# Sample keys in runs of 1 KB, scores by 64x32 products, cache loads on GpSimd's queue

## The chip, the cores and the metric

One NeuronCore of a Trainium2 chip runs the whole program as one launch. The metric is the device time of that launch in microseconds (us); lower is better. The kernel before has a median of 2021.78 us over three runs (2021.5 to 2022.62).

## What is computed

One step of a one-layer decoder for two groups of requests that share the weights: a prompt of 256 new tokens, and 8 sample requests of 8 tokens each. A layer is a mixer (retention beside a short gated convolution), cross-attention to 256 memory tokens, and a SwiGLU FFN, all in fp32 with a model width of 2048. The change touches only the cross-attention of the sample requests, whose memory keys and values come from a cache in DRAM:

```python
q = (h @ w_xq).reshape(B, T, XA_HEADS, XA_DIM)          # 4 heads of 512
s = einsum('bthd,bnhd->bhtn', q, mk) * XA_DIM ** -0.5   # mk, mv: (8, 256, 4, 512) from the cache
p = softmax(s)
o = einsum('bhtn,bnhd->bthd', p, mv)
x + o @ w_xo
```

For the prompt, mk and mv are products of the memory tokens with w_mk and w_mv, and are outputs too.

## The kernel before, in words

Every large product is done three times over on parts: a weight tile is loaded raw (SP's queue, 512 KB a load, L109), split into a high part by ACT (L121) and a remainder by DVE (L122), and multiplied as high x high, high x low and low x high (`mm3`, L162 to L165). `Weights` walks one list of all weight tiles, four raw buffers and five pairs of parts deep, with loads and splits three ahead. One call of its `next()` gives one *chunk*: 12 matmuls of 320 columns in most stages, 6 matmuls of 512 columns in the memory key and value products.

The order of all instructions on TensorE, ACT and DVE is written out by hand. Everything that is not a large product is a Python generator in the queue `background`. After each chunk, `tick(rate)` (L207) adds `rate` to a credit of at most two and runs the front generator for one step, that is to its next `yield`, per whole credit. `drain()` (L217) runs the queue to its end at once.

The cross-attention stage starts at L726. First the query product (8 groups of 8 chunks, rate RATE_XQ after the first group, L972 to L987), whose background is the norm table, `memory_tiles` (transposes of the prompt's memory, L779) and, from groups 1 and 3 on, `sample_head(0)` and `sample_head(1)`. Then, for each of four heads, the memory key and value products (16 chunks each, rate 1, L993 to L1008); heads 2 and 3 of the samples are appended at their own head, and the prompt's own attention of each head (`prompt_scores`, `prompt_values`, 8 and 5 steps) is put at the front of the queue. Last, 12 chunks of the output product (L1012), the drain (L1013) and the rest of that product, which needs the result of all heads.

`sample_head(h)` (L845) takes its requests in two halves p, of four requests j each. Per half: four key tiles (512 KB) are transposed in 32x32 blocks by DVE, one a step, each followed by `fetch_keys()`, which asks for the tile three places on; two empty steps; 16 score matmuls (L860), four requests side by side on column tiles of 32. After the second half the first four value tiles are asked for (`load_values`, L809), the exponents and their sums are made, three steps later the weights are transposed (L876), two steps later 16 value matmuls (L887) run; the second value tiles are asked for, and PACE = 5 steps later the second 16. Keys and values share four `kt` buffers, so a value load waits until the matmuls before have read the buffer. All of these loads are issued by SP, in one order with the weight loads. `OUT` is GpSimd (POOL), which issues the stores of results.

The key load puts partition 32i+q on 128 elements of the head dimension (i) and key q of 32: runs of 512 B.

Of the kernel before, what the change touches and what calls it, by code (L numbers as in the profile page):

```python
# [11 lines left out]
F32 = mybir.dt.float32  # L12
# [24 lines left out]
RATE_RET, RATE_XQ, RATE_KV = 0.9, 1.0, 1.0  # L37
PACE = 5
# [97 lines left out]
def step_kernel(ctx, tc, a, o):  # L136
# [15 lines left out]
    def uid(s):  # L152
        count[0] += 1
        return f"{s}_{count[0]}"
# [284 lines left out]
    with tc.tile_pool(name="ret", bufs=2, reuse_waits="tile") as ret:  # L439
# [162 lines left out]
        for pair in range(4):  # L602
# [27 lines left out]
            if pair == 0:  # L630
                loading.close()
                hold_b = ctx.enter_context(tc.tile_pool(name="hold_b", bufs=1, side="right",
                                                        reuse_waits="tile"))
                b_hi = hold_b.tile([P, KT, T], F32R, name="b_hi")
                b_lo = hold_b.tile([P, KT, T], F32R, name="b_lo")
                hold_b.tile([P, 120], F32, name="fill_b")
# [89 lines left out]
    with tc.tile_pool(name="att", bufs=1, reuse_waits="tile") as att:  # L726
        q_p = att.tile([P, KT, TP], F32, name="q_p")
        q_s = att.tile([P, KT, 80], F32, name="q_s")
        G.memset(q_s[:, :, 64:80], 0.0)
# [23 lines left out]
        def fetch_keys():  # L753


            if not key_order:
                return
            h, b = key_order.popleft()
            src = a["cache_mem_k"][0, b, :, h]
            t = att.tile([P, 8, P], F32, tag="keys", name=uid("keys"), bufs=3)  # L760
            for i in range(4):
                DMA.dma_start(out=t[32 * i:32 * i + 32],
                              in_=src[:, P * i:P * i + P].rearrange("(n q) d -> q n d", q=32))
            keys.append(t)
# [3 lines left out]
        def fetch_memory():  # L768


            i = mem_order.popleft()
            t = att.tile([P, 8, P], F32, tag="keys", name=uid("mem"), bufs=3)
            for d in range(4):
                DMA.dma_start(out=t[32 * d:32 * d + 32].rearrange("p (n m) d -> p n (m d)", n=2),
                              in_=a["mem_prompt"][0, 64 * i:64 * i + 64, XD * d:XD * d + XD]
                              .rearrange("(n q) d -> q n d", q=32))
            keys.append(t)

        def memory_tiles():  # L779
            for i in range(4):  # L780
                t = keys.popleft()
                kt = kv_tile().rearrange("p (n k q) -> p n k q", k=KT, q=32)
                V.transpose(out=kt, in_=t.rearrange("p (n m) d -> p n (m d)", n=2)  # L783
                            .rearrange("p n (c k) -> p n k c", k=KT))
                flat = t.rearrange("p (n m) d -> p n (m d)", n=2)
# [58 lines left out]

        def sample_head(h):  # L845
            ss = mix_tile()
            for p in range(2):
                kts = []
                for j in range(4):
                    kt = kv_tile().rearrange("p (n d c) -> p n d c", d=4, c=32)  # L850
                    V.transpose(out=kt, in_=keys.popleft().rearrange("p n (d c) -> p n d c", c=32))  # L851
# [13 lines left out]
            vs = load_values(h, 0)  # L865
            e, rc = exponents(ss, "s")
# [5 lines left out]
            for _ in range(3):  # L872
                yield
# [98 lines left out]
        for g in range(8):  # L972
            for i, ps in enumerate(product(a_hi, a_lo, KT, RATE_XQ if g else 1.0)):
                k = 2 * g + i
                V.tensor_tensor(out=q_p[:, k, :], in0=ps[:, 0:TP], in1=r_tab[:, 0:TP], op=ALU.mult)
                h, i = divmod(k, 4)
                for d in range(4):
# [14 lines left out]
        att.tile([P, 8], F32, name="fill_a")  # L992
        for h in range(XH):  # L993
            if h > 1:
                background.append(sample_head(h))
# [120 lines left out]
```

## Time and profile before

| what | value |
|---|---|
| median of three runs | 2021.78 us (2021.5 to 2022.62) |
| the profiled execution | 2018.07 us, of which the span in the trace is 2016.3 us |
| TensorE busy | 1985.9 us, 98% of the span |
| DVE, ACT, POOL busy | 1076.1 us (53%), 840.9 us (42%), 123.5 us (6%) |
| DMA | 340.94 MB, mean 169 GB/s |

A busy engine is one with an instruction in flight; matmuls are pipelined, so their recorded times overlap and a busy stretch need not run at full rate. Idle time is put down to what ended it. [...]

### The profile page before, as it was taken

To read this page: it belongs to the slowest core of one execution; us is meant where nothing else is said; L and a number is where in the kernel's file an instruction comes from. 1 tells how busy PE (TensorE), PEld (TensorE's weight loads), DVE (VectorE), ACT (ScalarE), POOL (GpSimd) and SP (SyncE) were. 2 spreads that over 40 slices of the span, in tenths; PEclk is the share of its full clock that TensorE was granted. 3 is DMA by queue.
4 is the path that set the end of the run, shared out by engine and by line. 5 is a ranking of instruction groups with operands and counts; after the bars stand their busy time and mean duration, and the time that the engine had idled before them with its cause. 6 is when DMAs were issued, how large, how long until landed. Compare 5 with 4: busy or idle time off the path is not lost.

```text
span 2016.3 us, 34017 instructions
## 1 busy us (share of the span) xinstructions
PE 1985.9 (98%) x13310; PEld 1907.1 (95%) x13310; DVE 1076.1 (53%) x1931; ACT 840.9 (42%) x1648; POOL 123.5 (6%) x230
## 2 busy tenths in 40 slices
PE   9999999999999999999999999999999999999997
PEld 8999999999998878778899999999999999999997
DVE  5556666555566545556454545544454544545433
ACT  6444433334454345444344434333343433334444
POOL 1111111110110000000010000000000000000010
PEclk9999999999999999999999999999999999999999
DMA  6465555445559965878545444444444444444443
GB/s 211 144 194 158 184 172 162 147 152 174 157 157 252 241 237 187 220 249 260 167 138 160 140 154 152 148 152 151 151 146 147 151 153 153 141 156 150 134 146 115
DMA packets 327664, 340.94 MB, mean 169 GB/s; under 512 B 13132, under 2 KB 296640, under 8 KB 327504
## 3 DMA queue, kind: packets, MB, share of 16 engines
q1 hardware_dynamic: 324240, 329.72, 53.1%
q0 software_dynamic: 3264, 9.05, 1.3%
q8 instruction: 104, 1.70, 0.4%
q14 instruction: 56, 0.46, 0.1%
HBM read 327.11 MB, written 11.61 MB: 168 GB/s over the span
## 4 chain that ended last, share of the span: by engine, by line
PE 92%; DMA 4%; DVE 2%; issue 1%; ACT 1%; SPq 0%; POOL 0%; POOLq 0%; DVEq 0%; ACTq 0%
PE acc L163 29%; PE acc L165 29%; PE acc L164 29%; DMA keys<-in_cache_mem_k_dram 2%; DMA kt<-in_cache_mem_v_dram 2%; PE mix L887 1%; PE mix L860 1%; DVE w_lo L122 1%; PE mix L375 0%; PE mix L165 0%; PE mix L163 0%; PE mix L164 0%; DVE kt L783 0%; DVE kt L851 0%; DMA x_tok<-in_x_prompt_dram 0%
## 5 line engine op out<-in xcount | busy, mean ns | idle before, releaser
L122 DVE TENSOR_TENSOR w_lo<-w_raw,w_hi 128x512 fp32r<-128x512 f32 x1072 | 711.6, 693 | 505.6 <-ACT w_hi L121 504.1
L121 ACT CAST w_hi<-w_raw 128x512 fp32r<-128x512 f32 x1072 | 631.2, 619 | 593.9 <-PE acc L164 520.9
L163 PE MATMUL acc<-a_hi,w_hi 128*128 128x320 f32 x2112 | 660.1, 313 | 3.4 <-ACT w_hi L121 3.1
L165 PE MATMUL acc<-a_hi,w_lo 128*128 128x320 f32 x2112 | 653.9, 310 | 0.7 <-DVE w_lo L122 0.7
L164 PE MATMUL acc<-a_lo,w_hi 128*128 128x320 f32 x2112 | 653.3, 309 | 0.0
L163 PE MATMUL acc<-b_hi,w_hi 128*128 128x320 f32 x1664 | 514.5, 309 | 0.0
L165 PE MATMUL acc<-b_hi,w_lo 128*128 128x320 f32 x1664 | 514.3, 309 | 0.0
L164 PE MATMUL acc<-b_lo,w_hi 128*128 128x320 f32 x1664 | 514.3, 309 | 0.0
L163 PEld LDWEIGHTS acc<-a_hi,w_hi 128*128 128x128 f32 x2112 | 397.1, 188 | 11.2 <-issue 5.3
L165 PEld LDWEIGHTS acc<-a_hi,w_lo 128*128 128x128 f32 x2112 | 397.2, 188 | 1.9 <-DVE w_lo L122 1.9
L164 PEld LDWEIGHTS acc<-a_lo,w_hi 128*128 128x128 f32 x2112 | 397.4, 188 | 0.8
L163 PEld LDWEIGHTS acc<-b_hi,w_hi 128*128 128x128 f32 x1664 | 312.4, 188 | 0.1
L164 PEld LDWEIGHTS acc<-b_lo,w_hi 128*128 128x128 f32 x1664 | 312.4, 188 | 0.0
L165 PEld LDWEIGHTS acc<-b_hi,w_lo 128*128 128x128 f32 x1664 | 312.4, 188 | 0.0
L298 POOL TENSOR_TENSOR sq_sum<-sq_sum,sq_t 128x320 f32<-128x320 f32 x43 | 38.3, 891 | 1125.7 <-ACT sq_t L297 1125.7
L164 PE MATMUL acc<-w_lo,b_hi 128*128 128x512 f32 x256 | 100.6, 393 | 3.3 <-DVE w_lo L122 3.3
L163 PE MATMUL acc<-w_hi,b_hi 128*128 128x512 f32 x256 | 102.5, 400 | 0.0
L165 PE MATMUL acc<-w_hi,b_lo 128*128 128x512 f32 x256 | 100.2, 391 | 0.0
L707 DVE TENSOR_TENSOR x_res<-x_res,acc 128x320 f32<-128x320 f32 x80 | 37.7, 486 | 74.9 <-PE acc L165 74.9
L163 PEld LDWEIGHTS acc<-w_hi,b_hi 128*128 128x128 f32 x256 | 48.4, 189 | 14.2 <-issue 5.0
L164 PEld LDWEIGHTS acc<-w_lo,b_hi 128*128 128x128 f32 x256 | 48.4, 189 | 13.4 <-DVE w_lo L122 4.4
L165 PEld LDWEIGHTS acc<-w_hi,b_lo 128*128 128x128 f32 x256 | 48.4, 189 | 10.4
(226 smaller groups left out, 1017.4 us busy)
## 6 DMA issues: line engine op xcount, KB each, us to landing
w_raw<-in_w_in_dram SPq DMA_DIRECT2D x112, 512.0 KB, 4.1
w_raw<-in_w_gate_dram SPq DMA_DIRECT2D x88, 512.0 KB, 4.1
w_raw<-in_w_up_dram SPq DMA_DIRECT2D x88, 512.0 KB, 4.3
w_raw<-in_w_down_dram SPq DMA_DIRECT2D x80, 512.0 KB, 3.3
w_raw<-in_w_mix_out_dram SPq DMA_DIRECT2D x32, 512.0 KB, 4.5
w_raw<-in_w_xq_dram SPq DMA_DIRECT2D x32, 512.0 KB, 5.0
keys<-in_cache_mem_k_dram SPq DMA_DIRECT2D x128, 128.0 KB, 5.2
kt<-in_cache_mem_v_dram SPq DMA_DIRECT2D x32, 512.0 KB, 7.5
```

The source lines that it names most:

```text
L121: self.nc.scalar.copy(out=hi, in_=src)
L122: self.nc.vector.tensor_tensor(out=lo, in0=src, in1=hi.bitcast(F32), op=ALU.subtract)
L163: PE.matmul(out, ah, bh, start=start, stop=False)
L164: PE.matmul(out, ah, bl, start=False, stop=False)
L165: PE.matmul(out, al, bh, start=False, stop=stop)
L298: G.tensor_tensor(out=sq, in0=sq, in1=t, op=ALU.add)
L707: V.tensor_tensor(out=x_res[:, m, :], in0=x_res[:, m, :], in1=ps[:, 0:T], op=ALU.add)
L860: PE.matmul(ss[32 * j:32 * j + 32, NM * p:NM * p + NM] .rearrange("q (n c) -> q n c", c=32), q_s[:, 4 * h + d, 16 * j:16 * j + 32], kts[j] ...
L887: PE.matmul(os[32 * j:32 * j + 32, :], pts[:, n, p, 32 * j:32 * j + 32], vs[j][:, n, :], start=(p == 0 and n == 0), stop=(p == 1 and n == ...
```

## The change

- A key tile is loaded in runs of 256 elements (1 KB): partition 64i+32s+q holds key half i, head-dimension half s, and key q of 32, with four groups m of 32 keys beside each other.
- The score product of a half becomes 64 matmuls, each on 64 rows and 32 columns of the array (8 pieces e of the head dimension, 2 key halves i, 4 requests j) with 128 columns streamed; the two key halves go to two PSUM banks. The queries are kept on 64 partitions per head, scaled by DVE at the start of a sample head and copied to the other 64 by ACT (the scaling by POOL at L982 goes). The softmax works on the two banks.
- Keys and values are asked for on POOL's queue instead of SP's.
- PACE goes; V_TICKS = 10 steps lie between each request for values and its use, and the value matmuls of a half are cut into two steps of eight.
- RATE_XQ is 1.15 instead of 1.0, and sample heads 2 and 3 enter the queue one head earlier.
- Two unused filler tiles go.

The diff, cut to its core:

```diff
-RATE_RET, RATE_XQ, RATE_KV = 0.9, 1.0, 1.0
-PACE = 5
+RATE_RET, RATE_XQ, RATE_KV = 0.9, 1.15, 1.0
+V_TICKS = 10
...
-        q_s = att.tile([P, KT, 80], F32, name="q_s")
-        G.memset(q_s[:, :, 64:80], 0.0)
+        q_s = att.tile([P, 16, 64], F32, name="q_s")
+        q_rep = att.tile([P, 528], F32, name="q_rep")
+        G.memset(q_rep[:, 512:528], 0.0)
...
-            t = att.tile([P, 8, P], F32, tag="keys", name=uid("keys"), bufs=3)
-            for i in range(4):
-                DMA.dma_start(out=t[32 * i:32 * i + 32],
-                              in_=src[:, P * i:P * i + P].rearrange("(n q) d -> q n d", q=32))
+            t = att.tile([P, 1024], F32, tag="keys", name=uid("keys"), bufs=3)
+            for i in range(2):
+                for s in range(2):
+                    at = 64 * i + 32 * s
+                    OUT.dma_start(out=t[at:at + 32].rearrange("q (m d) -> q m d", d=256),
+                                  in_=src[P * i:P * i + P, 256 * s:256 * s + 256]
+                                  .rearrange("(m q) d -> q m d", q=32))
...
-                DMA.dma_start(out=t, in_=a["cache_mem_v"][0, 2 * j + p, :, h]
+                OUT.dma_start(out=t, in_=a["cache_mem_v"][0, 2 * j + p, :, h]
...
+        def sample_exponents(pair):
+            mxs = [att.tile([P, 2], F32, tag=f"mxs{i}", name=uid("mx")) for i in range(2)]
+            sv = [ps[:, 0:256].rearrange("p (t n) -> p t n", n=P) for ps in pair]
+            for mx, v in zip(mxs, sv):
+                V.tensor_reduce(out=mx, in_=v, axis=AX.X, op=ALU.max, negate=True)
+            V.tensor_tensor(out=mxs[0], in0=mxs[0], in1=mxs[1], op=ALU.min)
...
+            for t in range(2):
+                for i, v in enumerate(sv):
+                    S.activation(out=e[:, t, P * i:P * i + P], in_=v[:, t, :], func=AF.Exp,
+                                 bias=mxs[0][:, t:t + 1], scale=1.0, accum_out=sm[:, i, t:t + 1])
...
         def sample_head(h):
-            ss = mix_tile()
+            mine, other = (slice(64 * i, 64 * i + 64) for i in (h // 2, 1 - h // 2))
+            V.tensor_tensor(out=q_rep[mine, 0:512].rearrange("p (e t) -> p e t", t=64),
+                            in0=q_s[mine, 8 * (h % 2):8 * (h % 2) + 8, :],
+                            in1=r_tab[mine, TP:T].unsqueeze(1).to_broadcast([64, 8, 64]),
+                            op=ALU.mult)
+            S.copy(out=q_rep[other, 0:512], in_=q_rep[mine, 0:512])
+            ss = [mix_tile() for _ in range(2)]
...
-                for d in range(4):
-                    for j in range(4):
-                        PE.matmul(ss[32 * j:32 * j + 32, NM * p:NM * p + NM]
-                                  .rearrange("q (n c) -> q n c", c=32),
-                                  q_s[:, 4 * h + d, 16 * j:16 * j + 32], kts[j][:, :, d, :],
-                                  start=(d == 0), stop=(d == 3), tile_position=(0, 32 * j),
-                                  skip_group_check=True)
+                for e in range(8):
+                    for i in range(2):
+                        half = slice(64 * i, 64 * i + 64)
+                        for j in range(4):
+                            PE.matmul(ss[i][32 * j:32 * j + 32, P * p:P * p + P]
+                                      .rearrange("q (m c) -> q m c", c=32),
+                                      q_rep[half, 64 * e + 16 * j:64 * e + 16 * j + 32],
+                                      kts[j][half, :, e, :], start=(e == 0), stop=(e == 7),
+                                      tile_position=(64 * i, 32 * j), skip_group_check=True)
             vs = load_values(h, 0)
-            e, rc = exponents(ss, "s")
+            e, rc = sample_exponents(ss)
...
-            for _ in range(3):
+            for _ in range(4):
                 yield
...
-            for _ in range(2):
+            for _ in range(V_TICKS - 4):
                 yield
             os = mix_tile()
             for p in range(2):
...
+                    yield
                 if p == 0:
                     vs = load_values(h, 1)
-                    for _ in range(PACE):
+                    for _ in range(V_TICKS):
                         yield
...
-                    S.copy(out=q_s[32 * i:32 * i + 32, 4 * h + d, 0:64],
-                           in_=ps[32 * d:32 * d + 32, TP:T])
-                if i == 3:
-                    for d in range(4):
-                        G.tensor_tensor(out=q_s[:, 4 * h + d, 0:64], in0=q_s[:, 4 * h + d, 0:64],
-                                        in1=r_tab[:, TP:T], op=ALU.mult)
+                    S.copy(out=q_s[at:at + 32, place + d, :], in_=ps[32 * d:32 * d + 32, TP:T])
...
-            if h > 1:
-                background.append(sample_head(h))
+            if 0 < h < 3:
+                background.append(sample_head(h + 1))
```

The first `yield` added at the value matmuls stands after the eight matmuls of one n, inside the loop over n.

## Rows read from the trace of the kernel before

**Rows 1.** The page, part 1: busy time, share of the span and instructions by engine.

```profile
PE 1985.9 (98%) x13310; PEld 1907.1 (95%) x13310; DVE 1076.1 (53%) x1931; ACT 840.9 (42%) x1648; POOL 123.5 (6%) x230
```

**Rows 2.** Table by stretches: from:to, length, busy by engine, PEclk, DMA share, GB/s.

```profile
616.00:704.00 88.00, 82.95 (x610) 71.39 (x609) 48.57 (x78) 33.89 (x89) 2.31 (x8) 1.00 0.97 248
...
1090.00:1980.00 890.00, 890.00 (x6078) 889.93 (x6077) 431.44 (x719) 347.21 (x633) 9.70 (x11) 1.00 0.47 149
```

**Rows 3.** Table by stretches, four holes of TensorE in the cross-attention stage.

```profile
602.00:605.00 3.00, 1.49 (x9) 0.96 (x8) 1.06 (x2) 2.87 (x10) 1.15 (x4) 1.00 0.45 128
635.00:638.00 3.00, 1.85 (x11) 1.33 (x10) 1.02 (x2) 2.88 (x9) 1.15 (x4) 1.00 1.19 203
...
694.00:699.00 5.00, 3.66 (x40) 2.09 (x35) 2.91 (x6) 3.29 (x11) 0.00 (x0) 1.00 1.13 219
...
834.00:849.00 15.00, 11.62 (x69) 8.35 (x67) 9.86 (x14) 4.34 (x9) 0.72 (x1) 1.00 1.15 238
```

**Rows 4.** Table by stretches, the five us behind the last of these holes.

```profile
849.00:854.00 5.00, 5.00 (x20) 4.21 (x20) 4.03 (x6) 2.49 (x4) 0.00 (x0) 0.66 1.10 283
```

**Rows 5.** TensorE's timeline around value bursts: start, length, instruction [idle before it].

```profile
649.80 0.31 PE L165 MATMUL acc<-a_hi,w_lo 128*128 128x320 f32 x1
...
...
657.62 0.41 PE L163 MATMUL acc<-a_hi,w_hi 128*128 128x320 f32 x1
...
666.37 0.31 PE L165 MATMUL acc<-a_hi,w_lo 128*128 128x320 f32 x1
...
668.53 0.41 PE L163 MATMUL acc<-a_hi,w_hi 128*128 128x320 f32 x1
...
706.81 0.31 PE L165 MATMUL acc<-a_hi,w_lo 128*128 128x320 f32 x1
...
713.39 0.50 PE L163 MATMUL acc<-w_hi,b_hi 128*128 128x512 f32 x1
...
873.68 0.39 PE L164 MATMUL acc<-w_lo,b_hi 128*128 128x512 f32 x1
873.90 0.39 PE L165 MATMUL acc<-w_hi,b_lo 128*128 128x512 f32 x1
...
879.94 0.50 PE L163 MATMUL acc<-w_hi,b_hi 128*128 128x512 f32 x1
...
966.85 0.31 PE L165 MATMUL acc<-a_hi,w_lo 128*128 128x320 f32 x1
...
970.25 1.90 PE L887 MATMUL mix<-kt,pts 128*32 128x512 f32 x10 [0.43 <-DMA kt<-in_cache_mem_v_dram]
972.83 0.66 PE L908 MATMUL mix<-ident,misc 128*128 128x128 f32 x4 [0.68 <-ACT misc L896]
```

**Rows 6.** SP's timeline: start, length, the issues of the last values.

```profile
959.93 1.99 SPq L813 DMA_DIRECT2D kt<-in_cache_mem_v_dram  x4
```

**Rows 7.** Groups of instructions on POOL: its DMA issues, busy us and mean ns.

```profile
L549 POOL DMA_DIRECT2D out_ret_s_dram<-sn x8 | 7.4, 924 | 73.4 <-DVE sn L545 73.4
L523 POOL DMA_DIRECT2D out_ret_p_dram<-sp x8 | 5.0, 622 | 19.0 <-ACT sp L522 19.0
...
L1007 POOL DMA_DIRECT2D out_mk_dram<-kv x4 | 3.0, 750 | 108.7 <-ACT kv L1006 108.7
```

**Rows 8.** DMA issues: queue, count, KB each, median us from issue to landing.

```profile
keys<-in_cache_mem_k_dram SPq DMA_DIRECT2D x128, 128.0 KB, 5.2
...
out_mk_dram<-kv POOLq DMA_DIRECT2D x4, 512.0 KB, 5.7
```

**Rows 9.** Table by stretches, while key loads land.

```profile
641.00:645.00 4.00, 4.00 (x28) 4.00 (x28) 2.81 (x7) 2.57 (x7) 0.00 (x0) 1.00 1.20 200
```

**Rows 10.** TensorE's timeline and one line's instructions: matmuls on column tiles of 32.

```profile
624.53 1.94 PE L860 MATMUL mix<-kt,q_s 128*32 128x256 f32 x32
...
88.58 0.65 PE L500 MATMUL mix<-s,qm 128*32 128x128 f32 x16
...
L802 PE MATMUL mix<-ssq_mem,own x8: 171/182/193, 611.6 to 611.7; 128*32 128x2 f32 x8
```

More of the change, by code (lines that the diff above doesn't have):

```diff
@@ L635, in step_kernel @@
                 b_lo = hold_b.tile([P, KT, T], F32R, name="b_lo")
-                hold_b.tile([P, 120], F32, name="fill_b")
             background.append(iter((None,)))
@@ L771, in fetch_memory @@
             i = mem_order.popleft()
-            t = att.tile([P, 8, P], F32, tag="keys", name=uid("mem"), bufs=3)
+            t = att.tile([P, 1024], F32, tag="keys", name=uid("mem"), bufs=3)
             for d in range(4):
-                DMA.dma_start(out=t[32 * d:32 * d + 32].rearrange("p (n m) d -> p n (m d)", n=2),
+                DMA.dma_start(out=t[32 * d:32 * d + 32].rearrange("p (n d) -> p n d", n=2),
                               in_=a["mem_prompt"][0, 64 * i:64 * i + 64, XD * d:XD * d + XD]
@@ L782, in memory_tiles @@
                 kt = kv_tile().rearrange("p (n k q) -> p n k q", k=KT, q=32)
-                V.transpose(out=kt, in_=t.rearrange("p (n m) d -> p n (m d)", n=2)
-                            .rearrange("p n (c k) -> p n k c", k=KT))
-                flat = t.rearrange("p (n m) d -> p n (m d)", n=2)
+                flat = t.rearrange("p (n d) -> p n d", n=2)
+                V.transpose(out=kt, in_=flat.rearrange("p n (c k) -> p n k c", k=KT))
                 for n in range(2):
@@ L843, in part @@
             return ap.rearrange("p (j r) -> p j r", r=r)[:, :, 8 * p:8 * p + 8]
-        def sample_head(h):
-            ss = mix_tile()
+        def sample_exponents(pair):
[4 more added lines that the diff above has]
+            V.tensor_tensor(out=mxs[0], in0=mxs[0], in1=mxs[1], op=ALU.min)
+            e = misc_tile().rearrange("p (t n) -> p t n", n=NM)
+            sm = att.tile([P, 2, 2], F32, tag="sms", name=uid("sm"))
+            for t in range(2):
+                for i, v in enumerate(sv):
+                    S.activation(out=e[:, t, P * i:P * i + P], in_=v[:, t, :], func=AF.Exp,
+                                 bias=mxs[0][:, t:t + 1], scale=1.0, accum_out=sm[:, i, t:t + 1])
+            rc = att.tile([P, 2], F32, tag="rcs", name=uid("rc"))
+            V.tensor_tensor(out=rc, in0=sm[:, 0, :], in1=sm[:, 1, :], op=ALU.add)
+            V.reciprocal(out=rc, in_=rc)
+            return e, rc
+        def sample_head(h):
+            mine, other = (slice(64 * i, 64 * i + 64) for i in (h // 2, 1 - h // 2))
[5 more added lines that the diff above has]
+            ss = [mix_tile() for _ in range(2)]
             for p in range(2):
@@ L849, in sample_head @@
                 for j in range(4):
-                    kt = kv_tile().rearrange("p (n d c) -> p n d c", d=4, c=32)
-                    V.transpose(out=kt, in_=keys.popleft().rearrange("p n (d c) -> p n d c", c=32))
+                    kt = kv_tile().rearrange("p (m e c) -> p m e c", e=8, c=32)
+                    V.transpose(out=kt, in_=keys.popleft().rearrange("p (m e c) -> p m e c", e=8, c=32))
                     fetch_keys()
@@ L976, in step_kernel @@
                 h, i = divmod(k, 4)
+                at, place = 64 * (h // 2) + 32 * (i // 2), 8 * (h % 2) + 4 * (i % 2)
                 for d in range(4):
-                    S.copy(out=q_s[32 * i:32 * i + 32, 4 * h + d, 0:64],
-                           in_=ps[32 * d:32 * d + 32, TP:T])
-                if i == 3:
-                    for d in range(4):
-                        G.tensor_tensor(out=q_s[:, 4 * h + d, 0:64], in0=q_s[:, 4 * h + d, 0:64],
-                                        in1=r_tab[:, TP:T], op=ALU.mult)
+                    S.copy(out=q_s[at:at + 32, place + d, :], in_=ps[32 * d:32 * d + 32, TP:T])
             if g == 1:
@@ L990, in step_kernel @@
             background.appendleft(sample_outputs(h, osb))
-        att.tile([P, 8], F32, name="fill_a")
         for h in range(XH):
-            if h > 1:
-                background.append(sample_head(h))
+            if 0 < h < 3:
+                background.append(sample_head(h + 1))
             for dst, prompt_part in ((o["mk"], prompt_scores), (o["mv"], prompt_values)):
```

## The prediction

> **What bounds the kernel now.** I read the page first: TensorE is busy for 98% of the span [rows 1], so only two things can move the time: what TensorE has to do, and the holes and stretched bursts in it. Next the table by stretches: the FFN stretch has no hole (890.00 of 890.00 us, 6078 matmuls, so 0.146 us each), while 616 to 704 us loses 5.05 of 88 us with the DMA engines at 0.97 [rows 2]. The change only touches the stage from 572 to 977 us (query product, memory keys and values, start of the output product), so I read that stage's holes one by one. Four of them are a split (ACT and DVE, L121 and L122) that came late because a key load, or a weight load behind it on SP's queue, came late: 1.51, 1.15, 1.34 and 3.38 us, together 7.38 [rows 3]. [...]
>
> The value bursts are the largest item, and busy time hides most of it. A clean burst of 16 recorded matmuls lets the main product go on 2.16 us after the last main matmul (666.37 to 668.53). Where the values are late, it dribbles: a few matmuls per landed tile, with ten left when the last one lands at 970.25, and each stretch counts as busy. From the last main matmul to the next it takes 649.80 to 657.62 = 7.82 us in head 0, 706.81 to 713.39 = 6.58 in head 1, 873.90 to 879.94 = 6.04 in head 2 [rows 5]. Less 2.16 each, that is 5.66 + 4.42 + 3.88 = 13.96 us. Head 3 pays at its second burst: 966.85 to 972.83 is 5.98 us against a clean 2.16 for the burst and 0.68 for the copy that follows (972.83 less 972.15), a loss of 3.14 [rows 5].
>
> **The change part by part.** *Values ten chunks ahead.* The first request of a head stood 3 + 2 = 5 chunks ahead of its use, the second PACE = 5. A chunk of the query product is 12 x 0.146 = 1.76 us; one of the memory products is 6 matmuls at 0.22 (873.68 to 873.90) = 1.3 [rows 5]. Five are 6.6 to 8.8 us, which is less than the loads need: the last tile of the last group lands 970.25 - 959.93 = 10.3 us after the first issue [rows 5, 6]. Ten chunks are 13 to 17.6 us (15.3 at 1.15 steps a chunk), so heads 0 to 2 lose this wait: -13.96.
>
> *The end of the stage.* A sample head had 12 + 3 + 2 + 5 + 2 = 24 steps and gets 12 + 4 + 6 + 2 + 10 + 2 + 2 = 38. All steps: 7 (table) + 17 (memory) + 4 x 38 + 4 x 13 (prompt parts) = 228. Steps on offer before the drain at L1013: 8 + 56 x 1.15 + 128 + 12 = 212.4, plus up to 2 saved. I walked the queue by hand in the order of the code: head 3 reaches its first value product at the last chunk, and its second request, the ten steps and the use fall into the drain. There, nothing stands between request and use, so TensorE waits for the whole load. Bounds: the fourth of POOL's issues begins 3 x 0.75 = 2.25 us after the first, and a POOL transfer of 512 KB lands after 5.7 us [rows 7, 8], 8.0 in all, or 5.7 if issue time is hidden; the same loads in the same place took 10.3. I take 9, nearest to the last, against the 3.14 paid now: +5.86 (bounds +2.56 and +7.16). A hole this long should also lower the granted clock as at 849 us: +1.7 (0 to 2.4) [rows 4].
>
> *Keys in runs of 1 KB.* While keys were landing in runs of 512 B the engines moved 200 GB/s at a share of 1.20 [rows 9]; the FFN's weights in rows of 1 KB move 149 at 0.47, or 317 at a full share [rows 2]. Half the pieces should take little over half the time. [...]
>
> *Loads on POOL's queue.* 128 key issues and 32 value issues leave SP, so weights no longer stand behind a key or value load that waits for its buffer; the hole at 602 us (weights behind a key load that waited for a transpose) goes. POOL gets these 160 issues beside 8 stores and the memory norm's power. A value request now waits on POOL for the score matmuls; behind it stand stores nobody needs for 16 chunks, and no key load of the same head. POOL's issues cost 0.62 us (128 pieces), 0.75 (256) and 0.92 (1024) [rows 7]; a key load has 128 pieces, so 0.62 and 2.5 us a tile. A key tile asked for at one transpose is needed three chunks later (4.4 us, at 1.46 between the two products), and 2.5 of issue plus 5.2 of landing [rows 8] is 7.7. The splits run three chunks ahead and cover most of the lateness. Of the 7.38 us of late splits I leave 2.5 (bounds 0 and 5.87, the three key holes): -4.88. The half-speed stretch goes with them: -1.7.
>
> *Scores.* 16 matmuls of 256 columns per turn become 64 of 128 columns on half the rows. Now the four column tiles run together: 32 records in 1.94 us, and 16 records of 128 columns in 0.65 [rows 10]. If both row halves also run together, eight at a time, the streamed columns per tile stay the same: +0.3 for 8 groups. If the halves take turns, the columns double; the two rows give (1.94 - 0.65) / (2048 - 512) = 0.84 ns per streamed column, 2048 x 0.84 = 1.7 us a group, +13.8 in all. No row shows a row-tiled matmul. I take the first, since eight small matmuls on column tiles started within 0.1 us [rows 10], so that starting 16 in a stream of 107 ns turns need not bind.
>
> *Value bursts cut in two.* Each extra cut costs the switch of tile shape: a clean burst of 16 takes 2.16 us where 4 x 512 columns at 0.84 ns are 1.72, so about 0.35 beyond the steady step. Heads 0 to 2 get two each, head 3 none (it runs in the drain): 6 x 0.35 = +2.1.
>
> *At nothing:* one DVE product and one ACT copy more per head, and exponents in four pieces with a fourth step of slack. They hide behind splits done ahead, as DVE is busy 48.57 of 88 us there [rows 2]; without that cover, some 2 us a head. POOL's 16 scalings leave; they were waited for by nobody.
>
> Sum: -13.96 - 4.88 - 1.7 + 5.86 + 1.7 + 0.3 + 2.1 = **-10.6 us** against the profiled execution of 2018.07 us (span 2016.3), which lies 3.7 us under the median; carried over to the median of 2021.78, **2011.2 us**.
>
> **The rivals.** *The row halves take turns* (+13.8 - 0.3): +2.9, 2024.7 us, no change that can be told, since 0.2% or 4 us is about what a measurement of this kernel can tell from none. For it: no row-tiled matmul is in the trace. Against: the column tiles do overlap. *POOL's issues are the bound, slower than before.* Between a head's first transpose and its eighth lie 9 chunks, 13.1 us, in which five tiles must be issued one after another. At 0.62 us an issue that is 12.4 + 5.2 = 17.6, and the 4.4 us of splits ahead just cover it. At the 0.92 of the costliest row it is 23.7, 6.2 us late per head, 25 in all in place of the 2.5: +11.9, 2033.7 us. It decides against the change from about 0.78 us an issue. For it: the sizes are near; against: the row nearest in pieces is 0.62, and heads 2 and 3 are split by prompt parts. [...] *All waits go and the end is short* (end +2.56, no lower clock, no key waits): -10.6 - 3.3 - 1.7 - 2.5 = -18.1, 2003.7 us. For it: a POOL transfer of this size lands in 5.7 us [rows 8]. *Values not ahead at all:* that is head 3, already in the sum.
>
> **How the numbers follow.** Forecast 0.60, all waits gone 0.14, halves in turn 0.14, POOL bound 0.12. The likeliest case's own range is 2006 to 2018 (end, clock, key waits at their bounds). The range 2003 to 2025 takes in the first three cases and leaves out POOL. Faster 0.74, same 0.14, slower 0.12.
>
> **What would show it.** Right: value bursts of heads 0 to 2 without dribble, TensorE holes of about 9 us just before the drain's transposes with a lowered clock behind, score groups near 1.9 us, key issues near 0.62 us, DMA well above 200 GB/s while keys land. Wrong: score groups of 3.6 us, DVE waiting for keys by over 4 us a head, POOL busy without a gap in the transposes, or head 3 done before the drain, which would add 5 us of gain.

## The result, and the profile after

The change makes the kernel slower: 2032.72 us (median of four runs, 2031.91 to 2034.46) against 2021.64 us (four runs of the kernel before in the same session), a ratio of 1.0061 with a 95% interval of 1.0045 to 1.0077, or about 12 us. The profiled execution after took 2031.91 us with a span of 2030.1, 13.8 us more than the 2016.3 of before.

In a table by stretches PEclk is the granted TensorE clock as a share of full speed, and the DMA share the mean busy share of the core's 16 DMA engines, whose records overlap, so that it can pass 1. The table after (from:to, length, busy by engine with instructions, PEclk, DMA share, GB/s) answers to [rows 2]:

```profile
616.00:704.00 88.00, 80.99 (x862) 73.73 (x861) 45.22 (x74) 34.47 (x90) 32.77 (x59) 0.96 0.80 231
704.00:820.00 116.00, 108.73 (x760) 83.72 (x760) 64.68 (x109) 51.03 (x109) 27.97 (x48) 0.99 0.78 225
820.00:936.00 116.00, 115.30 (x803) 90.33 (x802) 68.85 (x113) 56.37 (x111) 23.98 (x40) 1.00 0.76 238
936.00:1010.00 74.00, 67.70 (x523) 57.03 (x522) 33.52 (x63) 26.96 (x57) 9.05 (x12) 0.95 0.56 181
```

The first stretch was to lose its holes. It loses 7.01 us of 88 in place of 5.05, and its clock has fallen from 1.00 to 0.96, another 3.5 us of full-speed work. The DMA engines move less, 231 GB/s in place of 248, at a smaller mean share. Where keys are waited for their share is above 1 all the same, 1.02 from 626 to 640 us, and 1.16 before; after and then before:

```profile
626.00:640.00 14.00, 11.16 (x88) 10.06 (x90) 6.52 (x7) 1.24 (x2) 7.21 (x15) 0.89 1.02 230
```

```profile
626.00:640.00 14.00, 12.85 (x107) 11.69 (x99) 8.55 (x11) 5.70 (x14) 1.15 (x4) 1.00 1.16 249
```

TensorE's timeline after (start, length, instruction, [idle before it <- what ended it]) answers to [rows 5]:

```profile
662.12 1.06 PE L918 MATMUL mix<-kt,pts 128*32 128x512 f32 x8
665.07 1.06 PE L918 MATMUL mix<-kt,pts 128*32 128x512 f32 x8
...
972.45 1.92 PE L918 MATMUL mix<-kt,pts 128*32 128x512 f32 x16
979.33 3.22 PE L918 MATMUL mix<-kt,pts 128*32 128x512 f32 x4 [4.95 <-DMA kt<-in_cache_mem_v_dram]
982.77 3.70 PE L918 MATMUL mix<-kt,pts 128*32 128x512 f32 x12 [0.22 <-DMA kt<-in_cache_mem_v_dram]
987.14 0.66 PE L940 MATMUL mix<-ident,misc 128*128 128x128 f32 x4 [0.68 <-ACT misc L928]
```

Both foreseen things are there. Head 0's values are in place: two half bursts of 1.06 us each, and no dribble. Head 3's second values come in the drain: from 974.37 (the end of its first burst) to the transposes at 987.14 TensorE spends 12.77 us on a burst and a copy that take 2.6 when clean, 10.2 too many where before lost 3.14. The clock fell inside this burst, so what it cost is part of the 10.2 (stretches after):

```profile
980.00:983.00 3.00, 2.78 (x5) 0.36 (x4) 0.00 (x0) 0.00 (x0) 0.00 (x0) 0.50 0.88 307
...
986.00:989.00 3.00, 2.02 (x11) 1.25 (x10) 0.45 (x2) 1.17 (x4) 0.00 (x0) 1.00 0.00 0
```

What went the other way is the keys. The waits of DVE after (total us, times, longest):

```profile
DVE kt L879 <- DMA keys<-in_cache_mem_k_dram: 22.4, 13, 3.0
```

Before it was:

```profile
DVE kt L851 <- DMA keys<-in_cache_mem_k_dram: 13.9, 8, 2.8
```

The groups by line after (count, busy, mean ns of one, idle before):

```profile
L891 PE MATMUL mix<-kt,q_rep 64*32 64x128 f32 x1024 | 18.6, 276 | 3.8 <-DVE kt L879 3.6
...
L766 POOL DMA_DIRECT2D keys<-in_cache_mem_k_dram x128 | 70.0, 553 | 130.5 <-DVE kt L879 83.1
```

And the score products before:

```profile
L860 PE MATMUL mix<-kt,q_s 128*32 128x256 f32 x256 | 17.3, 383 | 0.5 <-DVE kt L851 0.4
```

The 64x32 score products are nearly as cheap as hoped, 18.6 us for 8 groups against 17.3, and POOL issues a key load in 0.553 us, even less than the 0.62 assumed. The DMA issues after (count, KB each, median us to landing), against [rows 8]:

```profile
keys<-in_cache_mem_k_dram POOLq DMA_DIRECT2D x128, 128.0 KB, 6.1
```

A key load lands after 6.1 us instead of 5.2, counted from the start of its issue. How the waits come about stands in the timelines after, around 635 us. First DVE:

```profile
626.12 1.25 DVE L879 STREAM_TRANSPOSE kt<-keys 128x1024 f32<-128x1024 f32 x1 [0.27 <-PE mix L891]
...
630.26 1.25 DVE L879 STREAM_TRANSPOSE kt<-keys 128x1024 f32<-128x1024 f32 x1 [2.32 <-DMA keys<-in_cache_mem_k_dram]
634.52 1.25 DVE L879 STREAM_TRANSPOSE kt<-keys 128x1024 f32<-128x1024 f32 x1 [3.01 <-DMA keys<-in_cache_mem_k_dram]
635.68 0.65 DVE L122 TENSOR_TENSOR w_lo<-w_raw,w_hi 128x512 fp32r<-128x512 f32 x1
638.36 1.25 DVE L879 STREAM_TRANSPOSE kt<-keys 128x1024 f32<-128x1024 f32 x1 [2.03 <-DMA keys<-in_cache_mem_k_dram]
...
640.70 0.75 DVE L1007 TENSOR_TENSOR q_p<-acc,r_tab 128x256 f32<-128x256 f32 x2
```

The transposes come 4.1 us apart: one round of the three key buffers takes 638.36 - 626.12 = 12.24 us. POOL's timeline in the same stretch:

```profile
627.66 1.09 POOL L766 DMA_DIRECT2D keys<-in_cache_mem_k_dram  x2 [1.11 <-DVE kt L879]
629.70 0.55 POOL L766 DMA_DIRECT2D keys<-in_cache_mem_k_dram  x1 [0.95 <-DMA keys<-in_cache_mem_k_dram]
630.42 0.55 POOL L766 DMA_DIRECT2D keys<-in_cache_mem_k_dram  x1 [0.17 <-issue]
```

The transpose that begins at 626.12 ends at 627.37 and frees a buffer, which these four issues fill. They begin 0.3 us later and end at 630.97, since one of them waits for an earlier key transfer to end; the tile is transposed at 638.36. So 7.94 us of the round, from the start of the last issue at 630.42, go by while the last load lands: the transfer, not the issuing, is the greater part of the loop. While a half's four tiles are taken, at 1.15 steps a chunk, one is wanted every 1.76 / 1.15 = 1.53 us; the loop gives one every 4.08. Who waits behind DVE stands in the timelines of ACT and then of TensorE:

```profile
641.15 1.71 ACT L1011 COPY q_s<-acc 32x64 f32<-32x64 f32 x8 [10.76 <-DVE q_p L1007]
642.88 0.62 ACT L121 CAST w_hi<-w_raw 128x512 fp32r<-128x512 f32 x1
645.17 1.28 ACT L860 ACT_TABLE_LOAD   x1 [1.67 <-DVE mx L855]
```

```profile
636.39 0.41 PE L165 MATMUL acc<-a_hi,w_lo 128*128 128x320 f32 x1 [2.69 <-DVE w_lo L122]
```

The split of 635.68 costs TensorE 2.69 us, and q_p at 640.70 keeps ACT's copies waiting for 10.76 us, with ACT's own splits behind them.

### The profile page after: what moved, and what is told of

Its sections match the earlier page's. It is cut to its first block, busy times and chain, and to the rows that moved or that the text cites. A ratio compares the mean times of both kernels' runs of the same rounds, so it can differ in the third digit from the quotient of the medians.

```text
span 2030.1 us, 35610 instructions
## 1 busy us (share of the span) xinstructions
PE 1992.1 (98%) x14078; PEld 1912.2 (94%) x14078; DVE 1081.8 (53%) x1947; ACT 845.5 (42%) x1668; POOL 211.7 (10%) x374
## 4 chain that ended last, share of the span: by engine, by line
PE 91%; DMA 3%; issue 2%; DVE 2%; ACT 1%; POOL 0%; SPq 0%; POOLq 0%; DVEq 0%; ACTq 0%
PE acc L163 29%; PE acc L164 28%; PE acc L165 28%; DMA keys<-in_cache_mem_k_dram 2%; PE mix L918 1%; PE mix L891 1%; DVE w_lo L122 1%; DVE kt L879 0%; PE mix L375 0%; ACT w_hi L121 0%; POOL keys L766 0%; DMA kt<-in_cache_mem_v_dram 0%; PE mix L165 0%; PE mix L163 0%; PE mix L164 0%
## 5 line engine op out<-in xcount | busy, mean ns | idle before, releaser
L163 PEld LDWEIGHTS acc<-a_hi,w_hi 128*128 128x128 f32 x2112 | 398.0, 188 | 11.3 <-ACT w_hi L121 6.6
L766 POOL DMA_DIRECT2D keys<-in_cache_mem_k_dram x128 | 70.0, 553 | 130.5 <-DVE kt L879 83.1
```

The lines of the kernel that those rows point to most:

```text
L163: PE.matmul(out, ah, bh, start=start, stop=False)
L766: OUT.dma_start(out=t[at:at + 32].rearrange("q (m d) -> q m d", d=256), in_=src[P * i:P * i + P, 256 * s:256 * s + 256] .rearrange("(m q) ...
```

## The experiments

Ratios are to runs of the kernel before on the same chip, taken beside them, with a 95% interval behind; 0.001 is 2.0 us. The theories: **1**, POOL's queue makes the key loop longer; **2**, 1.15 steps a chunk ask too densely; **3**, a load's 32 partitions, not its runs, set the rate; **5**, the filler tiles that went mattered.

### Which queue, which rate, which lead

**Both loads on SP again**, L766 and L817:

```diff
-                    OUT.dma_start(out=t[at:at + 32] ...
+                    DMA.dma_start(out=t[at:at + 32] ...
-                OUT.dma_start(out=t, in_=a["cache_mem_v"] ...
+                DMA.dma_start(out=t, in_=a["cache_mem_v"] ...
```

> The change with its key and value loads back on SP's queue, nothing else undone. Theory 1 (POOL's queue is what made the key waits grow: landing of 6.1 us against 5.2, at most eight loads under way): the holes at 619, 633, 709 to 725 us go, and it is 10 us or more faster than the change, about 2020. Theory 2 (the step rate of 1.15 asks for keys too densely) and theory 3 (the key transfers themselves, 32 partitions a load, are the limit, whatever the queue): within 4 us of the change, 2028 to 2037, with key waits of DVE still near 20 us; if weights now stand behind key loads again, some us slower.

1.0026 (1.0017 to 1.0036), 2025.5 us. Its DMA issues:

```profile
keys<-in_cache_mem_k_dram SPq DMA_DIRECT2D x128, 128.0 KB, 4.5
```

The same loads land after 4.5 us instead of 6.1, DVE's key waits fall to 12.5 us, and 1.0061 - 1.0026 is 7 us. Theory 1, which wanted 10 us or more, holds for that part and not for the rest.

**Only the keys on SP** (the first of the two lines):

> The change with the key loads alone on SP's queue and the values still on POOL's. Theory 1: as the run with both on SP, or better since values leave SP free: 10 us faster than the change. Theories 2 and 3: within 4 us of it.

1.0041 (1.0027 to 1.0056), 2027.9 us: 4 of the 7 us, at the edge of what theories 2 and 3 allow and far from theory 1's 10. The interval overlaps that of the run with both on SP, so the values' share is not shown.

**The rate**, `RATE_XQ` 1.15 to 1.0:

> The change with RATE_XQ back at 1.0. Theory 2 (two transposes fall into one chunk at 1.15): the key waits in 616 to 730 us shrink by 8 to 12 us, while 8 more steps fall into the drain, where head 3 now does more: 3 to 6 us dearer; sum 2025 to 2030. Theories 1 and 3: the waits shrink by less than 3 us, so the time is that of the change or up to 6 us above.

1.0046 (1.0030 to 1.0063), 2028.9 us, inside theory 2's range. Key waits are down from 22.4 to 17.1 us in all, but only from 14.9 to 12.2 in the 616 to 730 us for which theory 2 wanted 8 to 12 less and the others under 3. The interval holds both a small gain and none, so theory 2 is neither shown nor refuted.

**The lead**, `V_TICKS` 10 to 7:

> The change with V_TICKS = 7 in place of 10: by a walk through the queue of steps no step is left for the drain. The end of the stage then costs 3 us in place of 10.2 (-7), and the value bursts of heads 0 to 2, asked for 6 to 7 chunks ahead (9 to 12 us against about 10 that the loads need), give back 0 to 3 us: 2026 to 2029 by every theory of the key waits, since those stay.

1.0065 (1.0048 to 1.0082): no gain. A miss for all theories, and a useful one. The end is cured, as the last stretch shows:

```profile
936.00:1010.00 74.00, 73.84 (x465) 65.38 (x464) 36.68 (x62) 32.25 (x63) 6.28 (x8) 1.00 0.58 191
```

That is 6.1 us of idle time less than the change has there, and no lowered clock (1.00 in place of 0.95). But DVE's key waits rose from 22.4 to 30.6 us: with shorter leads the next head's keys are wanted sooner. That the one caused the other is read from the order of the steps, not tried by itself.

### The parts of the change alone

**Values without the keys' part:** the kernel before with the change's waits, cuts, rate and order of heads.

```diff
-RATE_RET, RATE_XQ, RATE_KV = 0.9, 1.0, 1.0
-PACE = 5
+RATE_RET, RATE_XQ, RATE_KV = 0.9, 1.15, 1.0
+V_TICKS = 10
...
-                    for _ in range(PACE):
+                    for _ in range(V_TICKS):
...
-            if h > 1:
-                background.append(sample_head(h))
+            if 0 < h < 3:
+                background.append(sample_head(h + 1))
```

> The part of the change that is not about keys: values ten steps ahead, the cut bursts, RATE_XQ 1.15 and the heads one earlier, on the kernel of before with its key runs of 512 B, its scores and all loads on SP. Theory 3 (the transport of the keys is the limit, and the 1 KB runs take only a fifth off it, landing 5.2 us to 4.5 on SP's queue): values -14, end of the stage +7, key waits several us above those of the change with its loads on SP (12.5 us of DVE), so 2025 to 2034. Theory 1 (POOL's queue alone did the harm): the time of the change with its loads on SP or below, 2012 to 2022.

0.9999 (0.9986 to 1.0011), 2019.5 us. So all of the loss lies in what this run leaves out: 0.0035 in the queue of the key and value loads, 0.0027 (5.5 us) in the layout, the scores and the tiles.

**The queue alone:** the kernel before, with keys and values issued by POOL (`DMA` to `OUT` at L762 and L813).

> The kernel before with its key and value loads on POOL's queue and nothing else: the queue part of the change alone. By the prediction (weights no longer stand behind a waiting load, holes of 7.4 us shrink to 2.5): 5 us faster, about 2015. Theory 1 in its new form (three key buffers in a loop, each emptied by DVE, then POOL's answer of 0.8 to 1.1 us and four issues of 0.55 us before the transfer; the longer loop sets the key rate): key landing rises from 5.2 to 6 us, DVE's key waits from 13.9 to over 20, 5 to 9 us slower, 2026 to 2030.

1.0066 (1.0049 to 1.0083), 2033.2 us: 13 us slower, by more than either theory said, and in theory 1's direction. Its table by stretches:

```profile
616.00:704.00 88.00, 78.93 (x564) 65.88 (x563) 43.36 (x65) 28.43 (x76) 44.10 (x77) 0.94 0.89 233
...
820.00:936.00 116.00, 106.57 (x579) 81.12 (x578) 65.60 (x100) 48.81 (x90) 38.75 (x64) 0.99 0.83 232
```

Its DMA issues:

```profile
keys<-in_cache_mem_k_dram POOLq DMA_DIRECT2D x128, 128.0 KB, 6.5
```

With nothing else changed, landing goes from 5.2 [rows 8] to 6.5 us, DVE's key waits from 13.9 to 29.0, and the first stretch loses 9.07 us instead of 5.05 [rows 2].

The expectation is wrong in one reading: its 0.8 to 1.1 us are POOL's idle time, not its answer, which comes 0.3 us after a transpose ends. Taking the trace tile by tile, where DVE waited for a key, a round of the buffers is 9.3 us in the kernel before (mean of 8 such tiles) and 11.2 in this run (13 tiles). From the first to the fourth issue it is 1.9 us in both; from the fourth issue to the last landing it is 5.5 and 7.1. So what the queue adds to the loop is landing, not issue time.

Why the loads land later is argued from a count and not tried. On SP's queue weights and keys are issued in one order; on POOL's the keys are issued beside the weights, and more of both are under way together. Of the 128 key loads, 19 were issued beside two or more weight loads that had not landed in the kernel before, 60 in this run, 41 in the change and 18 in the change with its loads on SP. Beside none, one, and two or more, the median landing is 3.6, 5.8 and 7.3 us before, and 3.5, 5.2 and 8.2 here: with the same company POOL's queue is hardly later. In the change it is later even so (4.2, 5.9 and 7.8 against 3.7, 4.7 and 7.1 on SP).

### What sets the key rate

**Runs of 512 B on POOL's queue** (the old four loads, each of 32 partitions and 8 runs a partition; the score products then take other numbers, the work is the same, here and in the runs with 128 partitions):

```diff
-            for i in range(2):
-                for s in range(2):
-                    at = 64 * i + 32 * s
-                    OUT.dma_start(out=t[at:at + 32] ...
+            for i in range(4):
+                OUT.dma_start(out=t[32 * i:32 * i + 32].rearrange("q (n d) -> q n d", d=P),
+                              in_=src[:, P * i:P * i + P].rearrange("(n q) d -> q n d", q=32))
```

> The change with the key loads in runs of 512 B again, on POOL's queue, in four loads of 32 partitions a tile as before; the keys land in other places, so the scores are those of other numbers. If run length sets the rate: key landing well above 6.1 us, DVE's waits for keys 30 us or more, 2037 to 2050. If the 32 partitions of a load or the eight loads under way set it: within 4 us of the change, 2028 to 2037.

1.0073 (1.0056 to 1.0090), 2033.0 us, with key waits of 22.5 us. Its DMA issues:

```profile
keys<-in_cache_mem_k_dram POOLq DMA_DIRECT2D x128, 128.0 KB, 5.9
```

Half the run length lands no later: 5.9 us with 512 B against 6.1 with 1 KB.

**128 partitions a load** (four loads, 128 KB each, one run of 1 KB per partition):

```diff
...
+            for n in range(2):
+                for s in range(2):
+                    at = 512 * n + 256 * s
+                    OUT.dma_start(out=t[:, at:at + 256],
+                                  in_=src[P * n:P * n + P, 256 * s:256 * s + 256])
```

> The change with the same four key loads of 128 KB a tile in runs of 1 KB from POOL, but each over 128 partitions with one run, not over 32 with four; scores are those of other numbers. Theory 3 (32 partitions a load limit the transport): landing falls from 6.1 to 4 us or less, more than 300 GB/s while keys land, DVE's key waits below 8 us, and 8 to 15 us faster than the change: 2017 to 2024. If only POOL's queue and its eight loads under way count: landing 5.5 us or more, within 4 us of the change.

1.0033 (1.0020 to 1.0046), 2025.7 us: 5.7 us faster than the change with the same bytes, runs, loads and queue. Its DMA issues:

```profile
keys<-in_cache_mem_k_dram POOLq DMA_DIRECT2D x128, 128.0 KB, 4.5
```

**The same on SP's queue:**

> As the run before it, with key and value loads on SP's queue. Theory 3: key waits all but gone, 2013 to 2020, with the end of the stage (10 us) and the query product's end holes left. Without theory 3: as the change with its loads on SP, 2022 to 2028.

1.0000 (0.9990 to 1.0009), 2018.8 us, landing after 3.9 us, key waits of 8.8 us. Theory 3 holds on both queues, for 5 to 6 us, and is smaller than it was thought to be: on POOL's queue it wanted landing of 4 us or less, key waits below 8 and 8 to 15 us, and got 4.5, 13.2 and 5.7; on SP's the time lies in its range, but the waits are not all but gone. Landing is 6.1 us with 32 partitions against 4.5 with 128 on POOL's queue, 4.5 against 3.9 on SP's; what holds the narrower loads up, no run shows.

**Two loads of 256 KB in place of four**, 128 partitions each:

> The change with two key loads of 256 KB a tile (128 partitions, two runs of 1 KB each) from POOL in place of four; scores are those of other numbers. Beside the four loads of 128 partitions (2025.7): if POOL's issues stand in the loop of the key buffers, two fewer take 1.1 us or more off a loop, and the key waits fall to 9 us or less: 2020 to 2024. If the issues are hidden: 2024 to 2029.

1.0013 (1.0004 to 1.0022), 2023.2 us, 0.0020 below the run with four loads. An issue now takes 0.724 us, so a tile 1.45 us instead of 2.2. That points to POOL's issues in the loop as well, if less clearly than hoped: key waits fall from 13.2 to 10.8 us, not to 9, and the larger loads land later (5.5 us).

**Two loads of a tile on SP, two on POOL** (`(DMA, OUT)[i].dma_start`):

> The change with two of a tile's four key loads on SP's queue and two on POOL's, values on POOL's. If the issues and the eight loads that a queue has under way make POOL slow: the loop gets shorter than on either queue alone, landing 5 us or less, and the time is at or below that with all keys on SP (2028), 2022 to 2028. If the 32 partitions of a load set the rate: as keys on SP, 2026 to 2030.

1.0040 (1.0025 to 1.0055), 2027.6 us: as with all keys on SP. The two halves of the same tiles land at different times:

```profile
keys<-in_cache_mem_k_dram SPq DMA_DIRECT2D x64, 128.0 KB, 5.0
keys<-in_cache_mem_k_dram POOLq DMA_DIRECT2D x64, 128.0 KB, 6.2
```

Two queues bring nothing over SP's alone (2027.9 us); the time lies in both ranges, so this does not tell the issues from the form of the loads.

### What the layout and the scores cost

**The filler tile.** The change drops `fill_b`, 480 bytes beside b_hi and b_lo. In the built program b_hi then starts at byte 188384 of a partition instead of 187904, that is at 480 modulo 512 instead of 0, and so does b_lo. The kernel before without that line alone:

```diff
-                hold_b.tile([P, 120], F32, name="fill_b")
```

> The kernel before without its filler tile fill_b alone (480 bytes beside b_hi and b_lo, in which the memory's keys and values are split). In the trace of the change, and of each of its variants but the one with values alone, a matmul of the memory products comes 0.235 us after the last, against 0.229 to 0.230 with the filler; 768 of them make 4.6 us. Theory 5 (the shifted place of b_hi and b_lo in SBUF does it): pitch 0.235, 4 to 8 us slower than before. Otherwise: pitch 0.229 and no difference within 2 us, and the new scores or their tiles are the cause.

The first and the last of 78 matmuls in a row in the memory products, from TensorE's timeline before:

```profile
773.06 0.39 PE L163 MATMUL acc<-w_hi,b_hi 128*128 128x512 f32 x1
...
790.54 0.39 PE L165 MATMUL acc<-w_hi,b_lo 128*128 128x512 f32 x1
```

And of 78 in this run:

```profile
775.90 0.39 PE L163 MATMUL acc<-w_hi,b_hi 128*128 128x512 f32 x1
...
793.86 0.39 PE L165 MATMUL acc<-w_hi,b_lo 128*128 128x512 f32 x1
```

17.48 / 77 = 0.2270 us against 17.96 / 77 = 0.2332. The change has the slow pitch too; the first and the last of 47 in a row, from its TensorE timeline:

```profile
760.16 0.39 PE L164 MATMUL acc<-w_lo,b_hi 128*128 128x512 f32 x1
...
770.88 0.39 PE L165 MATMUL acc<-w_hi,b_lo 128*128 128x512 f32 x1
```

10.72 / 46 = 0.2330. For 768 matmuls 0.0062 more is 4.8 us. The pitch is shown; the total is not: 1.0008 (0.9997 to 1.0019), that is 1.6 us and 3.8 at most, under the 4 to 8 that were expected. Where the rest went, no run shows.

**A filler of 24 numbers in the change:**

> The change with a filler of 24 numbers (96 bytes) where 120 stood: the whole 480 don't fit beside the larger score tiles. b_hi then stands at a multiple of 128 bytes, not of 512. Theory 5: if 128 is enough, pitch 0.229 and 4 to 8 us faster than the change (2024 to 2028); if only 512 will do, or by the other theories, the time of the change, 2030 to 2036.

1.0061 (1.0041 to 1.0080), pitch 0.2324 with b_hi at 384 modulo 512, against 0.2270 at 0: a multiple of 128 bytes is not enough. No run has the full 480 in the change.

**Exponents in two pieces**, on the change with its loads on SP (each piece then reads one of the two score banks alone, so the weights are other numbers):

```diff
-                for i, v in enumerate(sv):
-                    S.activation(out=e[:, t, P * i:P * i + P], in_=v[:, t, :], func=AF.Exp, ...
+                S.activation(out=e[:, t, :], in_=pair[t][:, 0:256], func=AF.Exp, ...
```

> The change with its loads on SP's queue and a head's exponents in two pieces of 256 columns in place of four of 128; each piece reads one bank alone, so the weights of the values are other numbers. If the four pieces hold up ACT's splits (the waits of TensorE for w_hi of 2.5 us at 647 and 720 us, and the lower clock behind them): these shrink to 1.5 us or less and the clock stays up, 3 to 6 us faster than 2025.5: 2019 to 2023. If not: 2024 to 2027.

1.0014 (1.0005 to 1.0024), 2021.8 us, in the range expected. By the ratios that is 0.0012 or 2.4 us below the change with its loads on SP; the two intervals overlap, but the medians are 3.6 us apart and the runs of the kernel before beside them agree (2019.7 and 2019.8). Its table by stretches, where the clock is 1.00 and 0.99 instead of the 0.98 and 0.97 of the run beside it:

```profile
616.00:704.00 88.00, 82.16 (x892) 75.55 (x892) 49.58 (x78) 35.60 (x89) 0.00 (x0) 1.00 0.80 241
704.00:820.00 116.00, 113.21 (x894) 87.45 (x893) 67.54 (x113) 52.90 (x108) 2.26 (x3) 0.99 0.80 238
```

### Versions that beat both

**Values alone, 9 steps, 5 for the last head, rate 1.15:**

> The values' part alone, as before in this study, with V_TICKS 9, and 5 for the last head, so that by the walk through the steps nothing is left for the drain. The end of the stage costs 3 us in place of 10 (-7 with its clock); heads 0 to 2 still ask 13 us or more ahead, except where chunks are short. If the tail is all that stands between the values' part and its gain: 2011 to 2014, against 2019.5 with ten steps for all. If the heads, one step closer, wait for keys instead (as V_TICKS 7 did): 2016 to 2020.

0.9975 (0.9965 to 0.9985), 2015.4 us, between the two expectations. The end is closed; DVE's key waits are 20.0 us, above the 16.6 with ten steps.

**The same with rate 1.0, 8 steps, 5 for the last head:**

> The values' part with RATE_XQ 1.0, V_TICKS 8 and 5 for the last head; two steps are left for the drain. Theory 2 (fewer key waits at a lower rate): holes before the memory products below those of the run beside it by 3 us or more, values of heads 0 to 2 clean but for 0 to 2 us: 2009 to 2014. Without it: 2014 to 2018.

0.9969 (0.9957 to 0.9981), 2015.0 us, with key waits of 14.3 us and two late value bursts. It does not stand apart from the run before it, as expected without theory 2.

**Whole bursts, rate 1.0, ten steps, six for the last head** (against the run with values alone, cut):

```diff
...
-                                  skip_group_check=True)
-                    yield
+                                  skip_group_check=True)
...
-                    for _ in range(V_TICKS):
+                    for _ in range(V_TICKS if h < 3 else 6):
```

> Values ahead on the kernel of before and nothing of the keys' part: RATE_XQ 1.0, heads one earlier, ten steps for heads 0 to 2 and six for the last, and the value bursts whole again, which frees 16 steps, so that by the walk none is left for the drain. The run with eight steps and cut bursts (2015.0) still lost 2.8 and 4.4 us where values were late at 727 and 936 us, and paid 2 x 1.3 us for a burst that costs 2.16 whole: 8 x 0.45 = 3.6 us. If those go and key waits stay near 14 us: 2005 to 2010. If ten steps only move the waits to the keys of the next head: 2012 to 2016.

0.9927 (0.9913 to 0.9941), 2006.55 us: 14.7 us faster than before. The profiled execution is the slowest of its five, 2011.52 us. A row of its table by stretches, and behind it one of its value bursts from TensorE's timeline:

```profile
616.00:704.00 88.00, 86.34 (x623) 76.77 (x623) 48.20 (x78) 36.35 (x98) 3.49 (x12) 1.00 0.91 239
```

```profile
660.31 1.92 PE L887 MATMUL mix<-kt,pts 128*32 128x512 f32 x16
```

Key waits are 11.3 us, and the first stretch loses 1.66 us of 88. One burst is still late:

```profile
934.97 2.17 PE L887 MATMUL mix<-kt,pts 128*32 128x512 f32 x6
937.79 1.90 PE L887 MATMUL mix<-kt,pts 128*32 128x512 f32 x10 [0.64 <-DMA kt<-in_cache_mem_v_dram]
```

What a cut costs can now be read. From the main matmul ahead to the next one behind, a whole burst takes 2.14 us here (mean of the seven that are in time; the late one takes 4.97), a half burst 1.29 in the change (mean of 12). Less the step of the main product that lies in each (0.15 to 0.23 us), two halves are 0.24 us dearer than a whole, 1.9 us for eight bursts in place of the 3.6 expected. The rest of the gain over the run before it comes with the late bursts that went and the 16 steps that became free; these were not tried apart.

## Why the prediction was wrong

**The step that failed is the queue**, "Loads on POOL's queue", -4.88, with -1.7 for the clock behind it, which is the 5.00 us of [rows 4] times 1 - 0.66. By the queue run alone it is +13 us on the kernel before, and +7 within the change; why it is less there, no run shows. Of the clock the half-speed stretch behind 849 us did go (0.50 from 850 to 853 us before, 1.00 from 820 to 936 us after), but 0.96 over 88 us and 0.99 over 116 in the two stretches ahead of it lose about 4.7 us of full-speed work. Two things in it failed. It took the 5.2 us that a load needs to land on SP's queue [rows 8] for POOL's queue, where the same loads need 6.5 (the queue run). And it had the lateness in its hands: 2.5 of issue plus 5.2 of landing is 7.7 us against the 4.4 after which a tile is needed (3 x 0.62 + 5.2 = 7.1, since landing counts from the start of the last issue). It then let the splits three chunks ahead "cover most of the lateness", as if a tile were late once. But three buffers form a loop; the tile after waits for the tile before, and the lateness adds up over the eight tiles of a head until the cover is spent. That the loop does it is read from the timelines and the lengths of the rounds; no run had a fourth buffer. One of the text's own signs of being wrong came true: DVE waited 22.4 us for keys, 5.6 a head. The hole at 602 us, which it put down to weights behind a key load, is still there after (1.93 us): ACT's split of 603.50 stands behind copies that waited 1.09 us for DVE's q_p, so leaving SP's order had little to free.

**The rate of the transfer** was read from a row in which keys and weights share the engines [rows 9], and put down to run length alone. The runs gained nothing: 5.9 us with 512 B and 6.1 with 1 KB on POOL's queue. What counted was how many partitions a load writes: 6.1 us with 32 and 4.5 with 128, both in runs of 1 KB on POOL's queue.

**The rival "POOL's issues are the bound"** named nearly the measured time (2033.7), by luck: the reason was half right. Its price of 0.92 us an issue did not come (0.553), and its threshold of 0.78 was wrong: it timed a row of five tiles once and left out the wait for landing in each round. Issues took 0.550 to 0.633 us throughout the change, and no later landing goes with DVE's work beside them: the key loads beside which DVE worked for half or more of the 1.5 us from the start of the issue landed after 5.9 us, the others after 6.4 (medians).

**Values ahead**, -13.96, was right: no dribble in heads 0 to 2. The change hides it, and the last version shows it: its eight bursts take 19.9 us, from the main matmul ahead to the next matmul behind, against 35.4 before, and it is 14.7 us faster, with fewer key waits beside. **The end**, +5.86 and +1.7, was right in sum: 10.2 us lost against 3.14 before, or +7, the lowered clock included. **Scores**, +0.3, was right in kind: the row halves run together, at 1.3 us more busy time than before. **The cut bursts**, +2.1, were somewhat dear: six at 0.24 are 1.4.

**At nothing** missed three times. The exponents in four pieces cost some 2.4 us, in one place with the cover gone that the text named (ACT, 1.67 us of waiting and 1.28 of table load ahead of them). The two fillers, listed in the change as unused, had no line at all; one of them holds b_hi at its place, worth 0.006 us a matmul in the memory products. And the higher rate and the earlier heads had none: values, the end with its clock, and the cuts were to bring -4.3 us together, and the run with values alone brought none. There TensorE's idle time outside the value bursts and ahead of the drain is 12.6 us against 6.8 before (gaps of over 0.3 us), with DVE's key waits at 16.6 against 13.9.

By the ratios the loss is 0.0035 for the queue, 0.0027 for layout, scores and tiles (of which 0.0012 exponents and up to 0.0019 the filler) and -0.0001 for values, end, rate and order together. These add up to 0.0061 because each is the difference of two runs in a row, so the sum proves nothing; what of the 0.0027 is neither exponents nor filler stays open.

## What to carry to other kernels

A load that refills one of a few buffers is priced by the round of the loop (free, issue, land, use) divided by the number of buffers (here 12.24 / 3 = 4.08 us a tile around 635 us), not by one latency against one slack; any microsecond added to the round is paid at every tile once the cover is spent (in the queue run 9.3 us became 11.2, and DVE's key waits of 13.9 us became 29.0). Before a load is moved to another queue, ask which loads it would then run beside, compare what loads of the same form need there to land, and move the queue alone in one run. An unused tile in a tuned kernel is a part of it (here 0.2270 us a matmul became 0.2332 without it): ask what stands beside it.

## What the runs showed of the hardware

- The same key loads, beside this kernel's weight loads, land after 4.5 us from SP's queue and 6.1 from POOL's (32 partitions), 3.9 and 4.5 (128 partitions), medians of 128.
- Key loads issued beside two or more weight loads under way land after 7.1 to 8.2 us, beside none after 3.5 to 4.2, whichever of the two queues issues them (medians in four kernels).
- A load of 128 KB that writes 128 partitions is 0.6 to 1.6 us sooner there than one that writes 32 with the same runs.
- Matmuls of 512 columns whose other operand starts at 480 or 384 modulo 512 bytes came every 0.2332 and 0.2324 us, at 0 every 0.2270. The products that stream b_hi itself (455 to 566 us) kept 0.147 us either way.
